# Partial-array products of a chunked scan gathered in four places a scan, and the scan's step sizes stored in another order in DRAM

## The chip, the core and the metric

The kernel runs on one core of a Trainium2 chip. The core has five engines with an instruction stream each: TensorE (PE in the profile, with its weight loads as PEld), VectorE (DVE), ScalarE (ACT), GpSimd (POOL), and SyncE (SP), whose stream issues most of the DMAs. An engine works through its stream in order; between engines, semaphores hold an instruction back until its inputs are there. PSUM, which the products are written to, is used here as eight banks of 128 x 512 float32. The metric is the device time of one execution in microseconds. The kernel before takes 1631.19 us, the median of three runs (1631.13 to 1631.39).

## What is computed

The reference is one inference step of a two-layer trunk: a Mamba-2 layer with a chunked state-space scan, and a layer of causal pooling. It takes 1024 new tokens of one prompt and 8 sequences of 8 tokens (the sample), 1088 tokens in all. The change touches the scan of the first layer and the work around it. Cut to what matters:

```python
def ssd_scan(x, dt, A, B, C, h0):          # T = 128 tokens a chunk, 8 groups of 4 heads
    acum = jnp.cumsum(dt * A, axis=2)       # cumulated step sizes within a chunk
    decay = jnp.where(mask, jnp.exp(acum[:, :, :, None] - acum[:, :, None, :]), 0.0)
    CB = jnp.einsum('bctgn,bcsgn->bctsg', C, B)
    xdt = x * dt[..., None]
    y_intra = jnp.einsum('bctsgr,bcsgrp->bctgrp', CB[..., None] * decay, xdt)
    chunk_states = jnp.einsum('bctgn,bctgr,bctgrp->bcgrpn', B, jnp.exp(acum[:, :, -1:] - acum), xdt)
    # h_c = exp(acum_end) * h_(c-1) + chunk_states_c
    y_inter = jnp.einsum('bctgn,bctgr,bcgrpn->bctgrp', C, jnp.exp(acum), h_prev)
    return y_intra + y_inter, h_final
...
mod = silu(c) @ ada_w[i] + ada_b[i]         # shift, scale, gate: the conditioning
gated = y * silu(z)                         # RMS norm over each group of 256 channels, then @ w_out
x = x + (1.0 + gate) * out
```

## The kernel before

Activations lie with channels on the 128 partitions and tokens along the free dimension. A large float32 product is done as three products of rounded parts (`mm1`, L180): high by high, high by low, low by high. 1088 tokens are cut into three pieces `CH` of 364, 364 and 360; one piece of one output tile over 8 input tiles is a *unit* of 24 products.

**The scan layer** (`ssd_layer`, L1458) runs eight scans, one for each group g of four heads. `scan_group` (L504) is a generator: each `yield` is a place where other work may be put between its steps. The other work comes from the generator `beside` (L1494): the projections of the groups in `BESIDE` (`proj_group`, L387; 12 units for one group), then the output product (`op_units`, L1523). `FILL[g]` says how many units follow each of the eleven steps of scan g. What a scan has left after eleven steps (`rest`) is drawn in the next scan, at its steps 0 and 3.

**One scan** has eight chunks of 128 tokens and a ninth, the sample's 64 tokens. They are named by what they call:

- `load_ac(c)` (L524) loads the cumulated step sizes of the group's four heads for chunk c to all 128 partitions (tile `acb`, two buffers), from the DRAM tensor `acd`. `acd` has the layout of the computation, 128 rows of 320: row 32 j + head holds chunks 2 j and 2 j + 1, so four heads of one chunk are four rows of 128 numbers with a step between them.
- `front(c)` (L534): ScalarE takes exponents from `acb`; TensorE makes C by B and three transposes into one bank `tr` (two buffers); VectorE makes the masked decay `M` and the scaled rows `xd`; ScalarE copies B's transpose (`Bt`).
- `states(c)` (L583): for a pair of chunks, two products into bank `S` (one buffer). Then twice in a row: GpSimd scales the last state (`hd`, L596) and VectorE adds the product (`h`, L597; L593 for the very first). The second state of a pair depends on the first.
- `rows(c)` (L600): the outputs of the pair into two banks `y`: products of `xd` and `M` (L609), and, where there is a state, of the state and `ea` (L613), each on half of the array's columns (128*64 in the profile), two heads side by side. VectorE adds them to the rows in place (`evac_y`, L578).
- `sample_inter` (L617): the sample's states, loaded by `load_h0`, times C on quarters of the columns (128*32; `Z`, L628, bank `S`). `back_sample` (L635): the sample's rows on 64*64 and 128*64 (L641, L644, banks `y`). `state_sample` (L656): the sample's new states on the full array (L663).
- The end: gating with z, sums of squares on quarters of the columns (`ms`, L708, bank `y`), logarithm and exponent on ScalarE, a store and a broadcast load of the factors, scaling and a store of the rows.

The step order is: `front(0)`; `front(1)`; then for each pair `states`, the next pair's first `front`, `rows`, a yield, the second `front`, a yield. The sample's Z comes with the last pair, and its rows one step later.

**The conditioning.** `ada_block` (L240) makes a block of 256 outputs: 16 instructions on quarters of the columns (L253, bank `tr`), a ScalarE copy, and after a yield a gathering product on the full array (L262). 16 of these blocks lie in the scans. `run` (L1236) plans 14 of them (`ada_plan`) to the projection units: block by block at tiles 1, 2 and 3 of each group, the first part after the second unit of the tile and the second part after the third. Two more go to the output product (`ada_late`). Their weights come through the same stream of tiles as the projection's weights, in the order of use (`items`).

**What sets the order.** The program names an order; a planner with a time model then puts each engine's instructions in the order in which their inputs are ready by that model, earlier lines of the program first. `issue_after(ins)` keeps what is traced in its block behind `ins` on that engine; `high_priority(n)` lets a block count as n places earlier; a manual dependency of class Sync makes an instruction wait for another one.

Of the kernel before, what the change touches and what calls it, by code (L numbers as in the profile page):

```python
# [50 lines left out]
FILL = (((1,) * 10 + (2,),) * 4 + ((1,) * 9 + (4, 5),) + ((3, 2, 2, 2, 2, 2, 2, 2, 2, 2, 3),) * 2 + ((2, 2, 2, 1, 1, 1, 1, 1, 2, 2, 1),))  # L51
# [46 lines left out]
class Build:  # L98
# [81 lines left out]
    def mm1(self, ps, w, k, act, ch, first, last):  # L180
        nc, (hi, lo), (ah, al), (a, n) = self.nc, w, act, ch
        nc.tensor.matmul(ps[:, :n], hi[:, k, :], ah[:, a:a + n], start=first, stop=False)  # L182
        nc.tensor.matmul(ps[:, :n], hi[:, k, :], al[:, a:a + n], start=False, stop=False)  # L183
        nc.tensor.matmul(ps[:, :n], lo[:, k, :], ah[:, a:a + n], start=False, stop=last)  # L184
# [55 lines left out]
    def ada_block(self, src):  # L240

# [56 lines left out]

    def ln_set(self, mm=None):

        ins = self.nc.scalar.preload_act_table_set("natural_log_exp_and_others")
        if mm is None:
            self.tc.keep_in_program_order(ins)
        else:
            self.tc.add_manual_dep(ins.ins, mm.ins.name, mybir.DependencyInfo(mybir.DependencyClass.Sync, mybir.DependencyReason.DATA), reason="ln_set")
# [81 lines left out]
    def proj_group(self, G):  # L387

        for ii in range(4):
# [17 lines left out]
            ada = self.ada_do(self.ada_plan[G["g"], ii]) if (G["g"], ii) in self.ada_plan else iter(())  # L407
            for c in range(3):
# [3 lines left out]
                if c:  # L412
                    next(ada, None)
# [25 lines left out]
    def dt_phase(self, ps):  # L439
# [33 lines left out]
        nc.sync.dma_start(self.acd, ac)  # L473
# [30 lines left out]
    def scan_group(self, g, T):  # L504
# [16 lines left out]
        h = [None]  # L521
        acbs = {}

        def load_ac(c):  # L524
            if c < 8:
                j, cc = c // 2, c % 2
                t = gp.tile([P, 4, 128], F32, tag="acb", bufs=2, name=self.name("acb"))
                nc.sync.dma_start(t, self.acd[32 * j + 4 * g:32 * j + 4 * g + 4, 128 * cc:128 * cc + 128].unsqueeze(0).to_broadcast([P, 4, 128]))
            else:
                t = gp.tile([P, 4, 128], F32, tag="acb", bufs=2, name=self.name("acb"))[:, :, :64]  # L530
                nc.sync.dma_start(t, self.acd[96 + 4 * g:100 + 4 * g, 256:320].unsqueeze(0).to_broadcast([P, 4, 64]))
            acbs[c] = t

        def front(c):  # L534
# [9 lines left out]
            pt = pp.tile([P, 512], F32, tag="tr", bufs=2, name=self.name("tr"))  # L544
            nc.tensor.matmul(pt[:L, 384:384 + L], B[:, tok], C[:, tok], start=True, stop=True)
            for i, t in enumerate((xs[0], xs[1], B)):
                o = pt[:, 128 * i:128 * i + 128]
                if c < 8:
                    nc.tensor.transpose(o, t[:, tok], self.ident)  # L549
                else:  # L550
                    self.dup(o, t[:, tok])
# [31 lines left out]
        def states(c, F):  # L583
# [5 lines left out]
            for i in range(2):  # L589
                cd, Si = F[i][5], S[:, 256 * i:256 * i + 256]  # L590
                hn = gp.tile([P, 4, 64], F32, tag="h", bufs=3, name=self.name("h"))
                if h[-1] is None:
                    nc.vector.tensor_copy(hn.rearrange("p r q -> p (r q)"), Si)  # L593
                else:
                    hd = gp.tile([P, 4, 64], F32, tag="hd", bufs=1, name=self.name("hd"))
                    nc.gpsimd.tensor_tensor(out=hd, in0=h[-1], in1=cd.unsqueeze(2).to_broadcast([P, 4, 64]), op=ALU.mult)  # L596
                    nc.vector.tensor_tensor(out=hn, in0=hd, in1=Si.rearrange("p (r q) -> p r q", r=4), op=ALU.add)  # L597
                h.append(hn)

        def rows(c, F):  # L600

            py = [pp.tile([P, 512], F32, tag="y", bufs=2, name=self.name("y")) for _ in range(2)]
            for i in range(2):
                tok, M, xdt, _, _, _, ct = F[i]
                hc, a = h[-3 + i], 128 * i
                for q in range(2):
                    for rr in range(2):
                        r, o = 2 * q + rr, slice(64 * rr, 64 * rr + 64)
                        nc.tensor.matmul(py[q][o, a:a + 128], xdt[:, r, :], M[:, r, :], start=True, stop=(hc is None))  # L609
                    if hc is not None:  # L610
                        for rr in range(2):
                            r, o = 2 * q + rr, slice(64 * rr, 64 * rr + 64)
                            nc.tensor.matmul(py[q][o, a:a + 128], hc[:, r, :], ct[:, r, :], start=False, stop=True)  # L613
            for q in range(2):
                evac_y(py[q], q, slice(128 * c, 128 * c + 256), 256)

        def sample_inter():  # L617

# [4 lines left out]
            nc.gpsimd.tensor_copy(mv[:, :, 1, 8:16], cv[:, :, 1, :])  # L623
            Z = pp.tile([P, 512], F32, tag="S", bufs=1, name=self.name("Z"))
# [5 lines left out]
            zsc = gp.tile([P, 4, 64], F32, tag="hd", bufs=1, name=self.name("zsc"))  # L630
# [4 lines left out]
        def back_sample(F, zsc):  # L635
            tok, M, xdt, xde, Bt, _, ea = F
            for q in range(2):
                py = pp.tile([P, 512], F32, tag="y", bufs=2, name=self.name("y"))
                for rr in range(2):
                    r, o = 2 * q + rr, slice(64 * rr, 64 * rr + 64)  # L640
                    nc.tensor.matmul(py[o, :64], xdt[:64, r, :], M[:64, r, :64], start=True, stop=False)  # L641
                for rr in range(2):
                    r, o = 2 * q + rr, slice(64 * rr, 64 * rr + 64)
                    nc.tensor.matmul(py[o, :64], zsc[:, r, :], self.kc[:, K_SEL64:K_SEL64 + 64], start=False, stop=True)  # L644
                evac_y(py, q, tok, 64)
# [28 lines left out]
        for c in range(0, 8, 2):  # L674
            states(c, F)
            if c == 6:
                load_z()
            Fn = [front(c + 2)]
            if c == 6:
                self.slots.free(B)  # L680
            rows(c, F)
            F = Fn
            if c == 6:
                zsc = sample_inter()
                self.slots.free(C)
# [6 lines left out]
        F, h = F[0], h[-1]  # L692
        nc.sync.dma_start(self.io["hpT"][g], h.rearrange("p r q -> p (r q)"))
        st = back_sample(F, zsc)
# [1112 lines left out]
```

## Time and profile before

| | |
|---|---|
| median of three runs | 1631.19 us |
| the profiled execution | 1633.98 us |
| its span, first to last instruction | 1632.2 us |
| granted TensorE clock over the span | 0.994 |
| projection and gating ahead of the scans | 0 to 354 us |
| the eight scans, with projection and output product beside them | 354 to 950 us |
| the rest | 950 to 1632 us |

How to read the profile: times are microseconds unless marked ns. L613 is line 613 of the kernel. `out<-in` names the tile that is written and those that are read, by the program's names. 128*64 is the part of the array that a product uses, rows by columns, and 128x128 the shape that it writes; a float32 product that is not split by the program shows as two instructions. Products are pipelined, so that two neighbours overlap, and the time that one takes is read from the distance of two starts. `<-` in a wait names what ended it.

### The profile page before, as it was taken

What the parts mean: (1) busy time and instruction counts of PE and PEld (TensorE: products, weight loads), DVE (VectorE), ACT (ScalarE), POOL (GpSimd) and SP (SyncE); (2) the same over time, 40 slices, a digit from 0 to 9 for tenths busy, and PEclk for the clock granted to TensorE, in tenths of its full rate; (3) what the DMA queues carried; (4) which work ended last, traced back from release to release, by engine and by line L of the source; (5) the groups of instructions that cost most, each with busy time, mean ns of one, the idle gap of its engine ahead of it and who ended that gap; (6) DMA issues with size and microseconds to landing.
All of it is one profiled execution on the core that took longest, in us unless ns stands there. A gap on an engine that the chain in (4) does not pass through costs nothing.

```text
span 1632.2 us, 30956 instructions
## 1 busy us (share of the span) xinstructions
PE 1601.1 (98%) x12061; PEld 1524.7 (93%) x12061; DVE 1290.3 (79%) x2140; ACT 816.7 (50%) x1565; POOL 495.2 (30%) x527
## 2 busy tenths in 40 slices
PE   8999999999999999999999999999999999999997
PEld 6899999998899888988998899999999999999997
DVE  6875779777788888789887867988889867577876
ACT  6653334456776767575645536632322333333364
POOL 0233556511221202121212222366667640000241
PEclk9999999999999999999999999999999999999999
DMA  9422232264555554668898533043333369565783
GB/s 346 163 98 84 93 109 71 105 203 133 183 162 167 165 186 135 217 232 299 276 332 284 201 137 111 29 142 112 102 112 99 129 213 367 166 170 173 167 164 119
DMA packets 122306, 275.60 MB, mean 169 GB/s; under 512 B 18192, under 2 KB 59312, under 8 KB 122160
## 3 DMA queue, kind: packets, MB, share of 16 engines
q1 hardware_dynamic: 118128, 260.91, 46.8%
q0 software_dynamic: 4032, 12.72, 4.5%
q8 instruction: 95, 1.56, 0.4%
q14 instruction: 51, 0.42, 0.1%
HBM read 201.12 MB, written 70.23 MB: 166 GB/s over the span
## 4 chain that ended last, share of the span: by engine, by line
PE 82%; DVE 7%; DMA 5%; issue 3%; ACT 2%; POOL 1%; SPq 0%; DVEq 0%; ACTq 0%; POOLq 0%
PE st L982 11%; PE st L980 11%; PE st L981 11%; PE mm L182 10%; PE mm L184 10%; PE mm L183 10%; DMA acb<-acd 2%; PE op L1197 2%; PE op L1198 2%; PE op L1196 2%; PE y L609 2%; PE S L588 2%; PE y L613 2%; PE am L253 1%; PE tr L549 1%
## 5 line engine op out<-in xcount | busy, mean ns | idle before, releaser
L982 PE MATMUL st<-hh,w 128*128 128x272 f32 x832 | 240.8, 289 | 2.3 <-DVE w L176 2.3
L980 PE MATMUL st<-hh,w 128*128 128x272 f32 x832 | 240.2, 289 | 0.0
L981 PE MATMUL st<-hl,w 128*128 128x272 f32 x832 | 239.7, 288 | 0.0
L982 PE MATMUL st<-t,w 128*128 128x272 f32 x624 | 179.6, 288 | 0.0
L980 PE MATMUL st<-t,w 128*128 128x272 f32 x624 | 179.6, 288 | 0.0
L981 PE MATMUL st<-t,w 128*128 128x272 f32 x624 | 179.2, 287 | 0.0
L182 PE MATMUL mm<-hh,wh 128*128 128x364 f32 (+1 forms) x528 | 178.4, 338 | 0.1
L184 PE MATMUL mm<-hh,wl 128*128 128x364 f32 (+1 forms) x528 | 174.6, 331 | 0.0
L183 PE MATMUL mm<-hl,wh 128*128 128x364 f32 (+1 forms) x528 | 173.7, 329 | 0.0
L174 ACT ACTIVATE w<-wr 128x512 fp32r<-128x512 f32 x104 | 65.6, 631 | 190.4 <-PE st L982 156.8
L982 PEld LDWEIGHTS st<-hh,w 128*128 128x128 f32 x832 | 156.4, 188 | 3.4 <-DVE w L176 3.4
L980 PEld LDWEIGHTS st<-hh,w 128*128 128x128 f32 x832 | 156.7, 188 | 0.3 <-issue 0.3
L981 PEld LDWEIGHTS st<-hl,w 128*128 128x128 f32 x832 | 156.8, 188 | 0.0
L596 POOL TENSOR_TENSOR hd<-h,cd 128x256 f32<-128x256 f32 x56 | 47.1, 842 | 353.6 <-DVE h L597 195.4
L182 PE MATMUL mm<-gh,wh 128*128 128x364 f32 (+1 forms) x384 | 130.2, 340 | 2.1 <-ACT raw L419 2.1
L1197 PE MATMUL op<-b,w 128*128 128x272 f32 x448 | 129.0, 288 | 1.3 <-DVE b L1126 1.3
L1198 PE MATMUL op<-b,w 128*128 128x272 f32 x448 | 129.0, 288 | 0.7 <-DVE w L1170 0.7
L1196 PE MATMUL op<-b,w 128*128 128x272 f32 x448 | 129.6, 289 | 0.0
L184 PE MATMUL mm<-gh,wl 128*128 128x364 f32 (+1 forms) x384 | 127.1, 331 | 0.0
L183 PE MATMUL mm<-gl,wh 128*128 128x364 f32 (+1 forms) x384 | 126.7, 330 | 0.1
L980 PEld LDWEIGHTS st<-t,w 128*128 128x128 f32 x624 | 117.7, 189 | 0.0
L982 PEld LDWEIGHTS st<-t,w 128*128 128x128 f32 x624 | 117.3, 188 | 0.0
(293 smaller groups left out, 4613.7 us busy)
## 6 DMA issues: line engine op xcount, KB each, us to landing
wr<-win SPq DMA_DIRECT2D x48, 512.0 KB, 3.7
acb<-acd SPq DMA_DIRECT2D x64, 256.0 KB, 3.9
wr<-pin SPq DMA_DIRECT2D x32, 512.0 KB, 3.6
wr<-pout SPq DMA_DIRECT2D x28, 512.0 KB, 3.9
x<-x1d SPq DMA_DIRECT2D x24, 544.0 KB, 6.3
x1d<-x SPq DMA_DIRECT2D x22, 544.0 KB, 5.4
wr<-pout POOLq DMA_DIRECT2D x20, 512.0 KB, 5.5
x<-xT SPq DMA_DIRECT2D x16, 544.0 KB, 6.0
```

Of the source, the lines that this page charges most:

```text
L174: self.nc.scalar.activation(hi, src, AF.Copy)
L182: nc.tensor.matmul(ps[:, :n], hi[:, k, :], ah[:, a:a + n], start=first, stop=False)
L183: nc.tensor.matmul(ps[:, :n], hi[:, k, :], al[:, a:a + n], start=False, stop=False)
L184: nc.tensor.matmul(ps[:, :n], lo[:, k, :], ah[:, a:a + n], start=False, stop=last)
L588: nc.tensor.matmul(S[:, 256 * i:256 * i + 256], Bt, xde.rearrange("p r q -> p (r q)"), start=True, stop=True)
L596: nc.gpsimd.tensor_tensor(out=hd, in0=h[-1], in1=cd.unsqueeze(2).to_broadcast([P, 4, 64]), op=ALU.mult)
L980: nc.tensor.matmul(ps[c][:, :QUART], hi[:, k], xh[:, t], start=(k == 0), stop=False)
L981: nc.tensor.matmul(ps[c][:, :QUART], hi[:, k], xl[:, t], start=False, stop=False)
L982: nc.tensor.matmul(ps[c][:, :QUART], lo[:, k], xh[:, t], start=False, stop=(k == 3))
L1196: nc.tensor.matmul(ps[:, :QUART], hi[:, k], xh, start=k == 0, stop=False)
L1197: nc.tensor.matmul(ps[:, :QUART], hi[:, k], xl, start=False, stop=False)
L1198: nc.tensor.matmul(ps[:, :QUART], lo[:, k], xh, start=False, stop=k == 7)
```

## The change

It has four parts.

1. *Places for the products on a part of the array.* `rows` becomes `visit`. It comes one yield after `states`, and holds, in one block with `high_priority(400)`: the row products of the pair, the first of which waits by a manual dependency for the later of the pair's two states, and behind the last of them (`issue_after`) whatever else of that kind there is. In visit 0 that is the sums of squares of the scan before (`next(rest)`), in visit 4 the sample's transposes, its C by B and Z, in visit 6 the sample's rows, and in visits 0, 2 and 6 of the first five scans a block of conditioning.
2. *What this moves.* The sample's front follows in the step of visit 4, before the last pair's states; its states are loaded at pair 2 instead of pair 4. B and C are freed there too. The sample's rows and the sums of squares go to bank `S`, the scaled Z to the tile `xl`. The second part of a conditioning block follows the next `states`. The end of a scan has two more yields, and is drawn at steps 0, 3 and 5 and in visit 0 of the next scan.
3. *The start of a scan.* From scan 1 on, the units of the first step come before the scan's first `front`, which is kept behind the last product of them, and in scans 1 to 4 the three units of the first three steps stand there together.
4. *The step sizes in DRAM.* `acd` becomes 8 chunks x 32 heads x 128, written by four DMAs, and the sample's part a tensor of its own, `acs`, written by a fifth. A load reads the four heads of a chunk as one run of 512 numbers for each partition.

```diff
-FILL = (((1,) * 10 + (2,),) * 4 + ((1,) * 9 + (4, 5),) + ((3, 2, 2, 2, 2, 2, 2, 2, 2, 2, 3),) * 2 + ((2, 2, 2, 1, 1, 1, 1, 1, 2, 2, 1),))
+FILL = ((1,) * 10 + (2,),) + (((3, 0, 0) + (1,) * 7 + (2,),) * 3 + ((3, 0, 0) + (1,) * 6 + (4, 5),) + ((3, 2, 2, 2, 2, 2, 2, 2, 2, 2, 3),) * 2 + ((2, 2, 2, 1, 1, 1, 1, 1, 2, 2, 1),))
+ADA = (0, 2, 6)
+HIGH = 400
...
+    def behind(self, ins, other):
+        self.tc.add_manual_dep(ins.ins, other.ins.name, mybir.DependencyInfo(mybir.DependencyClass.Sync, mybir.DependencyReason.DATA), reason="behind")
...
-        nc.sync.dma_start(self.acd, ac)
+        for j in range(4):
+            nc.sync.dma_start(self.acd[2 * j:2 * j + 2].rearrange("c h t -> h c t"), ac[32 * j:32 * j + 32, :256].rearrange("h (c t) -> h c t", c=2))
+        nc.sync.dma_start(self.acs, ac[96:128, 256:320])
...
-                nc.sync.dma_start(t, self.acd[32 * j + 4 * g:32 * j + 4 * g + 4, 128 * cc:128 * cc + 128].unsqueeze(0).to_broadcast([P, 4, 128]))
+                src = self.acd[c, 4 * g:4 * g + 4]
...
+            nc.sync.dma_start(t.rearrange("p r t -> p (r t)"), src.rearrange("r t -> (r t)").unsqueeze(0).to_broadcast([P, t.shape[1] * t.shape[2]]))
...
-        def rows(c, F):
+        def visit(c, F, F8=None, zsc=None):
             py = [pp.tile([P, 512], F32, tag="y", bufs=2, name=self.name("y")) for _ in range(2)]
...
+            with self.tc.high_priority(HIGH):
+                mm = None
+                for i in range(2):
...
+                            m = nc.tensor.matmul(py[q][o, a:a + 128], xdt[:, r, :], M[:, r, :], start=True, stop=(hc is None))
+                            if mm is None:
+                                mm = m
+                                self.behind(mm, hins[-1])
...
+                with self.tc.issue_after(m.ins):
+                    if c == 0:
+                        next(rest, None)
+                    if c == 4:
+                        self.pts = pp.tile([P, 512], F32, tag="tr", bufs=2, name=self.name("tr"))
+                        for i, t in enumerate((xs[0], xs[1], B)):
+                            self.dup(self.pts[:, 128 * i:128 * i + 128], t[:, NP:TOK])
+                        nc.tensor.matmul(self.pts[:64, 384:448], B[:, NP:TOK], C[:, NP:TOK], start=True, stop=True)
+                        Z = sample_products()
+                    if c == 6:
+                        _, M, xdt, _, _, _, _ = F8
+                        py8 = pp.tile([P, 512], F32, tag="S", bufs=1, name=self.name("y"))
...
+                    if (g, c) in self.ada_plan:
+                        self.ada = self.ada_do(self.ada_plan[g, c])
+                        next(self.ada)
...
         for c in range(0, 8, 2):
             states(c, F)
-            if c == 6:
+            next(self.ada, None)
+            if c < 6:
+                Fn = [front(c + 2)]
+            if c == 2:
+                load_h0()
+                sample_prep()
+            elif c == 6:
                 load_z()
...
             yield
             if c < 6:
-                F.append(front(c + 3))
+                zsc = visit(c, F)
+                Fn.append(front(c + 3))
+                F = Fn
                 if c == 4:
-                    load_h0()
+                    F8 = front(8)
+                    self.slots.free(B, C)
+            else:
+                py = visit(c, F, F8, zsc)
...
-        places = [(g, ii) for g in BESIDE for ii in (1, 2, 3) if (g, ii) != (BESIDE[-1], 3)]
+        places = [(g, c) for g in range(len(BESIDE)) for c in ADA]
...
             for i, n in enumerate(FILL[g]):
-                next(sc)
+                if i or not g:
+                    next(sc)
                 for j in range(n):
                     next(self.fill)
-                    if i in (0, 3) and j == 0:
+                    if i in (0, 3, 5) and j == 0:
                         next(rest, None)
+                if g and not i:
+                    with self.tc.issue_after(self.last_mm.ins):
+                        next(sc)
```

More of the change, by code (lines that the diff above doesn't have):

```diff
@@ L304, in ln_set @@
         else:
[L305 removed]
+            self.behind(ins, mm)
         return self.tc.issue_after(ins.ins)
@@ L633, in sample_inter, with back_sample @@
             return zsc
-        def back_sample(F, zsc):
+        def back_sample(F, py):
             tok, M, xdt, xde, Bt, _, ea = F
             for q in range(2):
[L638 to L645, printed above, removed]
+                evac_y(py[:, 64 * q:64 * q + 64], q, tok, 64)
             for i in range(2):
@@ L1479, in ssd_layer @@
         self.out_unit()
-        next(rest)
+        for _ in range(3):
+            next(rest)
         for _ in range(2):
```

95 lines of the change are left out of this document (50 added, 45 removed).

## The prediction

> **What bounds the kernel now.** I read the page first, for the engine that sets the time.
>
> ```profile
> span 1632.2 us, 30956 instructions
> PE 1601.1 (98%) x12061; PEld 1524.7 (93%) x12061; DVE 1290.3 (79%) x2140; ACT 816.7 (50%) x1565; POOL 495.2 (30%) x527
> ```
>
> TensorE is busy for 98% of the span, so time is gained only by giving TensorE less to do or less to wait for. The diff touches the eight scans, from 354 to 950 us, so next I cut that part into scans, and asked what TensorE waited for there (columns of the first view: stretch, its length, busy time and instructions of PE, PEld, DVE, ACT, POOL, clock, DMA share, GB/s).
>
> ```profile
> 435.00:510.40 75.40, 75.40 (x588) 67.78 (x586) 61.88 (x95) 51.49 (x116) 13.72 (x27) 1.00 0.51 167
> 882.00:950.00 68.00, 63.49 (x479) 57.57 (x479) 51.57 (x102) 33.52 (x79) 11.28 (x12) 0.97 0.59 204
> PE S L588 <- ACT Bt L566: 4.5, 3, 2.3
> PE mm L182 <- ACT raw L419: 2.1, 1, 2.1
> PE y L613 <- DVE h L593: 1.4, 1, 1.4
> ```
>
> The first row is scan 1, with TensorE busy all through; the second is scan 7. All its waits in the eight scans are three groups, 8.0 us: one at the first products of scan 0, one at the end of scan 4, three in scan 7. But a busy TensorE is not at its peak, so I went on to the timeline, where the distance between two starts shows what a product really takes (columns: start, duration, then the instruction; x8 is eight merged).
>
> ```profile
> 449.56 0.33 PE L184 MATMUL mm<-hh,wl 128*128 128x364 f32 x1
> ...
> 453.06 0.33 PE L184 MATMUL mm<-hh,wl 128*128 128x364 f32 x1
> ...
> 458.94 0.32 PE L183 MATMUL mm<-hl,wh 128*128 128x364 f32 x1
> 459.19 0.66 PE L613 MATMUL y<-ea,h 128*64 128x128 f32 x8
> 459.78 0.43 PE L184 MATMUL mm<-hh,wl 128*128 128x364 f32 x1
> 460.05 0.33 PE L182 MATMUL mm<-hh,wh 128*128 128x364 f32 x1
> ...
> 469.01 0.39 PE L613 MATMUL y<-ea,h 128*64 128x128 f32 x4
> 469.23 0.39 PE L609 MATMUL y<-M,xd 128*64 128x128 f32 x4
> ```
>
> From 449.56 to 453.06 lie 21 full-array products: 3.50 / 21 = 0.167 us each. In the middle of a long stretch of half-array products four of them take 469.23 - 469.01 = 0.22 us, so eight take 0.44. The eight at 459.19 stand alone in a run of full-array products, and the border shows three times: they start 0.25 after L183 instead of 0.167 (0.085 lost), take 0.59 instead of 0.44 (0.15 lost), and the first full product after them takes 0.27 instead of 0.167 (0.10 lost). **A stretch of products on a part of the array costs about 0.34 us by its two borders**, whatever is in it, and TensorE counts as busy meanwhile.
>
> **How many stretches.** Here is scan 1, which runs from one set of sums of squares (L708) to the next, by the first row of each stretch.
>
> ```profile
> 435.20 0.67 PE L708 MATMUL ms<-z,ones 128*32 128x272 f32 x8
> 444.44 0.65 PE L609 MATMUL y<-M,xd 128*64 128x128 f32 x6
> 445.65 0.87 PE L609 MATMUL y<-M,xd 128*64 128x128 f32 x10
> 446.82 0.66 PE L613 MATMUL y<-ea,h 128*64 128x128 f32 x8
> 454.72 0.44 PE L609 MATMUL y<-M,xd 128*64 128x128 f32 x4
> 459.19 0.66 PE L613 MATMUL y<-ea,h 128*64 128x128 f32 x8
> 461.14 1.07 PE L253 MATMUL am<-wr,scp 128*32 128x256 f32 x16
> 468.74 0.44 PE L609 MATMUL y<-M,xd 128*64 128x128 f32 x4
> 479.36 1.07 PE L253 MATMUL am<-wr,scp 128*32 128x256 f32 x16
> 481.42 0.27 PE L545 MATMUL tr<-xbc,xbc 128*64 128x64 f32 x1
> 489.55 0.33 PE L641 MATMUL y<-M,xd 64*64 64x64 f32 x4
> 499.71 1.07 PE L253 MATMUL am<-wr,scp 128*32 128x256 f32 x16
> ```
>
> That is 12. Counted the same way along the timeline, scan 0 has 11, scans 1 to 3 have 12 each, scan 4 has 11, scan 5 has 11 (its first pair alone is in four), scans 6 and 7 have 6 each, and the squares of the last scan stand alone: 11 + 36 + 11 + 11 + 12 + 1 = 82, from the first row here to the last.
>
> ```profile
> 366.65 0.66 PE L609 MATMUL y<-M,xd 128*64 128x128 f32 x8
> ...
> 942.07 0.67 PE L708 MATMUL ms<-z,ones 128*32 128x272 f32 x8
> ```
>
> **The change part by part.**
>
> *Gathering.* After it, each scan has four visits, 32 in all. The squares go into the next scan's first visit, the conditioning products (L253) into visits 0, 2 and 6 of scans 0 to 4 (15 blocks, 14 before), the sample's transposes and Z into visit 4, the sample's products (L641, L644) into visit 6. Outside stay the squares of scan 7 and one late conditioning block: 34 stretches. No product is added or dropped. Removed: 82 - 34 = 48 borders, 48 x 0.34 = **-16.3 us**.
>
> *Changes of shape inside a visit.* A visit that goes from halves (128*64) to quarters (128*32) pays there. Before, this already happens once a scan, between the row products and Z:
>
> ```profile
> 483.45 0.48 PE L609 MATMUL y<-M,xd 128*64 128x128 f32 x4
> 483.67 0.48 PE L613 MATMUL y<-ea,h 128*64 128x128 f32 x4
> 484.08 1.07 PE L628 MATMUL Z<-h,ctm 128*32 128x256 f32 x16
> 485.08 0.43 PE L182 MATMUL mm<-hh,wh 128*128 128x360 f32 x1
> ```
>
> Four halves take 0.22 (483.45 to 483.67), the last four 0.41; part of the 0.19 is the tail that any stretch pays at its end, and I take 0.13 as the price of the change. New ones: three in each of scans 0 to 4 (squares and conditioning have the same shape), one in each of scans 5 to 7: 18 x 0.13 = **+2.3 us**. The sample's products are now entered from halves instead of from the full array; at 0.05 each, between nothing and the price of a change, 8 x 0.05 = **+0.4 us**. Bounds for both: 0 and 18 x 0.19 + 8 x 0.13 = 4.5.
>
> [...]
>
> *Waiting for the last state.* The first product of a visit waits for the later of the pair's two states (`behind`), and all the rest of the visit, and every full product issued after it, queues behind it on TensorE. Before, only L613 waited, and for the earlier state. The states of the pair at 453 us come at
>
> ```profile
> 458.36 0.41 DVE L597 TENSOR_TENSOR h<-hd,S 128x256 f32<-128x256 f32 x1
> 461.18 0.41 DVE L597 TENSOR_TENSOR h<-hd,S 128x256 f32<-128x256 f32 x1
> ```
>
> so the row products of that pair move from 454.72 to after 461.6. What covers this is the projection beside the scan, 4.0 us a unit (24 x 0.167), which the planner places ahead because it is ready; the visit's priority only brings it forward once its inputs are planned to be there. From 420 to 700 us the waits of TensorE have no row at all, with L613 placed in the middle of a unit (459.19) as soon as its state was done, so the planner's times hold against VectorE's. The evictions (L580) come later by the same 7 us; states do not read them, so the next pair doesn't wait. I take **0**, with bounds 0 and one POOL and one DVE step a visit (below).
>
> *Scan starts.* Scans 1 to 7 now have their fill of the first three steps first and then two fronts, the states and a third front. Units are the same in number: 12 in scans 1 to 3, 18 in scan 4. The front's loads and ScalarE work can run under those units (12 us). I take 0; without that cover a scan would stand for one landing, 3.9 us.
>
> *PSUM and slots.* The squares, the sample's rows and Z share the one bank "S" with the states; the next states come two units, 8 us, later, and between them lies one evicting step of ScalarE or VectorE. The load of the sample's states moves two steps ahead on SP's queue, past two loads of step sizes; if a slot is late, these and ScalarE queue behind it. Cover: each of those loads is issued a chunk ahead. 0; without it one landing, 3.9 us, once.
>
> *Step sizes in DRAM.* The store is five issues in place of one, in the front, before the scans begin: 0. Each load reads 2 KB in one run a partition instead of four of 512 B.
>
> ```profile
> acb<-acd SPq DMA_DIRECT2D x64, 256.0 KB, 3.9
> hpT<-h SPq DMA_DIRECT2D x8, 128.0 KB, 3.0
> ACT cd L574 <- DMA acb<-acd: 9.6, 3, 4.9
> ```
>
> A landing takes 3.9 us; a transfer of half the bytes in runs of 1 KB takes 3.0, so I expect 3.0 to 3.9. This pays only in scan 7, where ScalarE waits for these loads (last row, 846 to 950 us) and TensorE then for ScalarE, three times: 0 to 3 x 0.9 = 2.7 us less. I take the middle, **-1.3 us**. [...]
>
> **Sum.** -16.3 + 2.3 + 0.4 - 1.3 = -14.9 us. The profiled execution took 1633.98 us (1632.2 of it span), so 1619; the median of the runs is 2.8 below it, so **1616 us**.
>
> **The rivals.** *Visits that are a little late.* The borders (12 x 0.34 = 4.1 us in scan 1) have so far given VectorE time to get a state done; with fewer of them this slack shrinks. At 0.25 us a visit, 32 x 0.25 = 8: 1624. For it: VectorE is busy 61.9 of 75.4 us in order; against it: the empty list of waits.
>
> *Slower: every visit waits for the second state.* Place: the new wait of a visit's first product. Price: if TensorE reaches it when the first state is done, it stands for the second's GpSimd and VectorE steps, 0.61 (POOL row below) + 0.41 = 1.0 us, 32 x 1.0 = 32: 1616 + 32 = 1648. It decides above 14.9 / 32 = 0.47 us a visit. For it: the two states above are 2.8 us apart. Against: TensorE has other ready work, and the wait is planned.
>
> ```profile
> 458.85 0.61 POOL L596 TENSOR_TENSOR hd<-h,cd 128x256 f32<-128x256 f32 x1 [8.97 <-DVE h L597]
> ```
>
> *Not gathered.* The planner still puts full products between the parts of a visit, since conditioning waits for its weights and row products for their own inputs. With two of three removed borders back, -16.3 becomes -5.4 and the sum -4; with all back, 1631. Against it: every extra is tied behind the visit's last row product. I put 1629.
>
> *The old waits go too.* If the 4.5 in scan 7 disappear, and with them its slow clock (0.97 of 68 us, 2 us), and the waits of 2.1 and 1.4: 10.0 instead of 1.3, so 1607. Against it: they come from loads and an eviction that the change hardly touches.
>
> **How the numbers follow.** Forecast 0.60; a little late 0.20; slower 0.08; not gathered 0.06; old waits gone 0.06. The range goes from 1608 to 1628: it takes in the forecast with its bounds (-16.3 + 4.5 = -11.8 at one end, -16.3 - 2.7 = -19 at the other, so 1612 to 1619), the late visits up to 0.4 us each, and most of the last case. A change under 0.2%, 3.3 us, can't be told from none. Faster: 0.60 + 0.20 + 0.06 and a third of "not gathered", 0.88; within: 0.04; slower: 0.08.
>
> **What would show it.** In the profile after: about 34 stretches, scans 1 to 3 shorter by 8 x 0.34 - 3 x 0.13 = 2.3 us each, 73.1 instead of 75.4, with TensorE still busy throughout and no row for waits of L609 on L597 or L593; the same spacing of 0.22 for four halves; loads of step sizes landing in under 3.9. A row "L609 waits for h" of over 8 us would show the late visits, of over 15 the slower case. Wrong would be the forecast if scans 1 to 3 stayed at 75 us with no wait shown: then the borders are not what costs.

## The result

The changed kernel takes 1645.88 us, the median of four runs (1644.65 to 1652.7), beside 1631.29 us before (1631.13 to 1633.79): a ratio of 1.0094 with a 95% interval from 1.0065 to 1.0124. Forecast were 1616 us. The ratios below leave out three executions that were far slower than the others of their kernel: one of `e3` (1692.9 us), one of `e10` (5458.9 us) and one of the kernel before (2208.6 us). The profiled execution took 1652.7 us, slower than the median; a reading of where its extra 7 us lie follows below. First its page, the span and the busy times:

```profile
span 1650.9 us, 30957 instructions
PE 1601.8 (97%) x12061; PEld 1532.4 (93%) x12061; DVE 1297.2 (79%) x2140; ACT 812.4 (49%) x1564; POOL 505.3 (31%) x527
```

TensorE has as many products as before (12061) and is as long busy (1601.1 us before), in a longer span (1632.2 us before): it waits. The waits of TensorE in the scans after the change (total, times, longest):

```profile
PE y L622 <- DVE h L605: 14.8, 16, 2.2
PE S L596 <- ACT Bt L574: 6.9, 5, 2.1
PE mm L184 <- DVE gs L812: 1.4, 1, 1.4
PE S L701 <- ACT xs L698: 1.0, 1, 1.0
PE S L596 <- DVE zsc L676: 0.5, 1, 0.5
PE mm L184 <- ACT raw L423: 0.3, 1, 0.3
```

That is 24.9 us instead of 8.0, and the first row is new: L622 is the first product of a visit (L609 before), L605 the later state (L597 before). Scans 1 to 3, from one set of sums of squares to the next, in the same view as before:

```profile
460.80:541.90 81.10, 78.83 (x590) 71.28 (x586) 63.35 (x95) 50.83 (x118) 18.39 (x27) 0.94 0.47 156
541.90:618.90 77.00, 74.54 (x590) 67.75 (x586) 62.93 (x95) 50.49 (x118) 18.57 (x27) 1.00 0.51 165
618.90:697.00 78.10, 75.83 (x590) 69.23 (x586) 63.02 (x95) 50.75 (x118) 18.39 (x27) 0.98 0.49 162
```

Each of them was 75.4 and was to become 73.1. Counted along the timeline as before, there are 34 stretches of products on a part of the array, exactly as forecast. So the gathering was done, and it did not pay.

**Where the wait comes from.** The longest waits stand at the last visit of a scan. This is scan 1 after, TensorE, with the wait in brackets:

```profile
494.33 0.44 PE L622 MATMUL y<-M,xd 128*64 128x128 f32 x4 [1.95 <-DVE h L605]
...
495.25 0.39 PE L622 MATMUL y<-M,xd 128*64 128x128 f32 x4
495.47 0.47 PE L629 MATMUL y<-ea,h 128*64 128x128 f32 x4
495.72 0.65 PE L622 MATMUL y<-M,xd 128*64 128x128 f32 x4
496.15 0.65 PE L629 MATMUL y<-ea,h 128*64 128x128 f32 x4
```

VectorE in the same microseconds, in its order:

```profile
487.16 0.68 DVE L570 TENSOR_TENSOR xd<-tr,tkx 128x512 f32<-128x512 f32 x1
487.76 1.62 DVE L568 TENSOR_TENSOR M<-M,cb 128x512 f32<-128x512 f32 x1
489.31 2.43 DVE L583 TENSOR_TENSOR ea<-xbc,ea 128x512 f32<-128x512 f32 x1
...
492.72 0.40 DVE L605 TENSOR_TENSOR h<-hd,S 128x256 f32<-128x256 f32 x1
...
493.85 0.42 DVE L605 TENSOR_TENSOR h<-hd,S 128x256 f32<-128x256 f32 x1 [0.53 <-POOL hd L604]
```

And GpSimd:

```profile
486.89 4.29 POOL L685 TENSOR_TENSOR h<-h,ea 128x1024 f32<-128x1024 f32 x2
493.20 0.61 POOL L604 TENSOR_TENSOR hd<-h,cd 128x256 f32<-128x256 f32 x1 [2.02 <-DVE h L605]
```

The two operations `M` and `ea` take 0.69 us each where nothing lies beside them (rows of `e3` below), and here 1.62 and 2.43. They lie beside the two scalings of the sample's states on GpSimd (L685, 486.89 to 491.18), and the last pair's states, which follow in VectorE's order, come 2.7 us late. `xd`, which reads one input from PSUM, took its usual 0.68 beside the same work (0.67 to 0.69 in all 72). Each of the two slow ones ends shortly after a scaling: the scalings take 1.94 and 2.39 us, and `M` ends at 489.38, 0.55 us after the first, and `ea` at 491.74, 0.56 us after the second. What holds the two back until then is not shown by a row.

Before, the same scaling started when the last states were done (481.60 and 482.75 in the rows of VectorE). GpSimd and VectorE of the kernel before:

```profile
485.29 4.52 POOL L647 TENSOR_TENSOR h<-h,ea 128x1024 f32<-128x1024 f32 x2 [0.26 <-issue]
```

```profile
481.60 0.42 DVE L597 TENSOR_TENSOR h<-hd,S 128x256 f32<-128x256 f32 x1 [0.70 <-PE S L588]
482.75 0.42 DVE L597 TENSOR_TENSOR h<-hd,S 128x256 f32<-128x256 f32 x1 [0.73 <-POOL hd L596]
...
486.03 1.98 DVE L575 TENSOR_TENSOR ea<-xbc,ea 128x512 f32<-128x512 f32 x1
```

An `ea` beside it took 1.98 us there too, and ended 0.54 us after the first scaling (2.18 us, to 487.47), but nothing of the running pair came after it. The change traces the sample's front in the step of visit 4, so its `ea`, which the scaling needs, is ready before the last pair's states instead of behind them.

**The clock.** In the visit above, four products follow each other at 0.22 us (495.25 to 495.47) and then at 0.43 (495.72 to 496.15). A window of the kernel after from the wait on shows a granted clock of 0.58:

```profile
494.30:506.50 12.20, 12.17 (x87) 10.10 (x88) 7.82 (x13) 5.93 (x15) 1.36 (x4) 0.58 0.60 188
```

About 10 us at half clock followed this wait (12.20 x 0.42 / 0.5), and shorter pieces followed those of scans 3 and 4 (a clock of 0.98 over scan 3, and of 0.83 from 730 to 740 us). The wait alone does not bring it: the one of 1.97 us in scan 2 of this execution was followed by full clock (1.00 over the scan), and so were the three of 1.95 and 1.96 us in scans 1 to 3 of `e2` (below; 0.995 over its span). In the other three runs the mean clock is 0.991 to 0.994 instead of 0.988, and they are 6 to 8 us faster: the time of the profiled execution above the median goes with these pieces.

### The profile page after: what moved, and what is told of

The parts are those of the page before. It is cut to its first block, busy times and chain, and to the rows that moved or that the text cites. A ratio compares the mean times of both kernels' runs of the same rounds, so it can differ in the third digit from the quotient of the medians.

```text
span 1650.9 us, 30957 instructions
## 1 busy us (share of the span) xinstructions
PE 1601.8 (97%) x12061; PEld 1532.4 (93%) x12061; DVE 1297.2 (79%) x2140; ACT 812.4 (49%) x1564; POOL 505.3 (31%) x527
## 4 chain that ended last, share of the span: by engine, by line
PE 74%; DVE 11%; DMA 5%; issue 5%; ACT 3%; POOL 1%; SPq 0%; DVEq 0%; ACTq 0%; POOLq 0%
PE st L1027 11%; PE st L1025 11%; PE st L1026 11%; PE mm L185 8%; PE mm L184 8%; PE mm L186 8%; PE op L1242 2%; PE op L1243 2%; PE op L1241 2%; PE y L622 1%; DMA gr<-gyd 1%; DMA wr<-win 1%; PE am L256 1%; DVE M L568 1%; PE y L629 1%
## 5 line engine op out<-in xcount | busy, mean ns | idle before, releaser
L185 PE MATMUL mm<-hl,wh 128*128 128x364 f32 (+1 forms) x528 | 177.8, 337 | 0.0
L184 PE MATMUL mm<-hh,wh 128*128 128x364 f32 (+1 forms) x528 | 177.3, 336 | 0.0
L604 POOL TENSOR_TENSOR hd<-h,cd 128x256 f32<-128x256 f32 x56 | 52.1, 930 | 280.8 <-DVE h L605 139.9
L184 PE MATMUL mm<-gh,wh 128*128 128x364 f32 (+1 forms) x384 | 129.2, 338 | 1.7 <-DVE gs L812 1.4
```

## The experiments

Ratios are to the kernel before, run in turn on the same chip, with 95% intervals.

**The layout alone, and all but the layout.** `e1_layout_only` puts the new stores, loads and DRAM tensors of the step sizes into the kernel before. `e2_old_layout` puts the old ones into the kernel after, the same lines the other way round.

```diff
# e1, in the kernel before
-        nc.sync.dma_start(self.acd, ac)
+        for j in range(4):
+            nc.sync.dma_start(self.acd[2 * j:2 * j + 2].rearrange("c h t -> h c t"), ...)
+        nc.sync.dma_start(self.acs, ac[96:128, 256:320])
```

> The kernel before with only the new order of the step sizes in DRAM (store and loads). Collision theory (GpSimd's scaling of the sample's states, planned ahead of the last pair's states, slows VectorE beside it and holds visit 6 up by 2 us a scan) and wait theory (any visit pays for waiting for the later state): the layout is not the cause, so within 3 us of before, 1628 to 1634. Layout theory (loads of step sizes land in 4.6 us instead of 3.9 and make the fronts late): slower by 5 us or more, landing over 4.3.

> The changed kernel with the old order of the step sizes in DRAM. Collision and wait theory: within 4 us of the changed kernel, 1642 to 1650, visit 6 still waiting about 2 us in scans 0 to 4. Layout theory: 1640 or less.

Measured: 1.0000 [0.9989, 1.0011] and 1.0081 [1.0062, 1.0100]. The layout costs or brings nothing beyond the 1.8 us of its interval. On the page of the kernel after, the median load (`acb<-acd`) lands in 4.6 us, where it took 3.9 before: the landing became longer, not shorter. In the old program the new layout lands in 4.1 (`e1`), and in the new program the old layout lands in 4.7 (`e2`). So the rest of the change moved it, not the length of the runs; that it is the place of the loads in time is not shown.

**The scaling of the sample's states kept behind the last pair's states.**

```diff
# e3, in the kernel after: hds collects the instructions of L604
-            for i in range(2):
-                nc.gpsimd.tensor_tensor(out=h0[i], in0=h0[i], ...)
+            with self.tc.issue_after(hds[-1].ins):
+                for i in range(2):
+                    nc.gpsimd.tensor_tensor(out=h0[i], in0=h0[i], ...)
```

> The changed kernel with GpSimd's two scalings of the sample's states kept behind the last pair's second scaling on GpSimd's queue. Collision theory: the waits of visit 6 in scans 0 to 6 (12.4 us in the profile) go, and the half clock behind them, so 1633 or less, down to 1626. Wait theory: the list of waits of L622 for the states stays at over 12 us and the time over 1642.

Measured: 1.0028 [1.0010, 1.0045], so about 11 us of the 15 are gone with one line on GpSimd's order (the median, 1634.61, is 1.6 above what the collision theory allowed). VectorE of `e3` at the same place in scan 1:

```profile
484.62 0.69 DVE L568 TENSOR_TENSOR M<-M,cb 128x512 f32<-128x512 f32 x1
485.21 0.69 DVE L583 TENSOR_TENSOR ea<-xbc,ea 128x512 f32<-128x512 f32 x1
```

TensorE's waits for the later state fall from 14.8 to 4.0:

```profile
PE y L622 <- DVE h L605: 4.0, 11, 0.8
```

The collision is shown as the cause of most of the loss. It is moved rather than gone: the scalings now lie beside a rounding of weights (`wl`, L142, at 490.33), which takes 2.59 us in place of 1.22, and no wait of TensorE on it is shown. But with the states clear of it the kernel is still not faster than before, and scans 1 to 3 are where they were, with full clock:

```profile
457.70:532.90 75.20, 74.63 (x590) 67.89 (x586) 61.48 (x95) 50.61 (x118) 17.86 (x27) 1.00 0.49 169
532.90:608.60 75.70, 74.67 (x590) 67.83 (x586) 61.76 (x95) 50.37 (x118) 18.06 (x27) 1.00 0.51 168
608.60:683.80 75.20, 74.56 (x590) 67.88 (x586) 61.62 (x95) 50.59 (x118) 17.86 (x27) 1.00 0.50 168
```

So 226.1 us for the three instead of 226.2 with 24 stretches fewer, and 1.7 us of waits in them. That is close to what the prediction named as the sign that borders are not what costs, scans 1 to 3 at 75 us with no wait shown. The gain of the gathering itself is missing, and the other runs ask for it.

**No wait for the later state.**

```diff
# e4, in the kernel after
-                                self.behind(mm, hins[-1])
+                                pass
```

> The changed kernel without the manual wait for the later state, so that a product waits for its own inputs alone. Wait theory: the 14.8 us of waits go and the gathering stays worth 14, 1622 or less. Collision theory: the products of the second chunk still need the first state of the pair, which is late by the same collision, so only one step of GpSimd and VectorE (1.1 us) is saved in each of seven scans, about 1638, with some visits split.

Measured: 1.0213 [1.0196, 1.0231], 20.1 us of waits, 109 stretches. The time, 1665.52 us, is far above what either theory allowed. Without the wait the planner takes the visits apart; the wait is what keeps them whole, and it costs less than it saves.

**The wait for the earlier state.** `e5_first_state` is `e3` and `e7_first_only` the kernel after, each with this edit:

```diff
-                                self.behind(mm, hins[-1])
+                                self.behind(mm, hins[-2])
```

> The kernel with the late scaling (e3) where a visit waits for the earlier of the pair's two states, which is the only new state that its products read. Theory that the added wait is one step of GpSimd and VectorE too long: the 4.0 us of waits of L622 for the states fall under 1.5 and visits stay whole (34 to 40 stretches), 1631 or less. Rival, that the gathering needs the later state: visits split again, over 45 stretches, 1636 or more.

> The changed kernel, scaling not moved, where a visit waits for the earlier state. Collision theory: VectorE reaches the earlier state 1.1 us sooner than the later one, so the 2.0 us waits of visit 6 in scans 1 to 4 fall to 0.9 and the time to 1637 to 1641. Theory that the choice of state is the whole cause: 1633 or less.

Measured: 1.0019 [1.0003, 1.0034] and 1.0091 [1.0062, 1.0120]. With the collision still there nothing is won: the wait for the state shrinks to 2.0 us and `S <- Bt` grows to 14.8. With the states clear of the collision (`e5`) their row is down to 1.0, and a new one stands there:

```profile
PE y L645 <- DVE h L605: 4.1, 1, 4.1
```

The sample's rows (L645) share bank `S` with the states and wait until the later state has been read from it.

**The old fill.** `e6_old_fill` is `e3`, and `e8_first_old_fill` is `e5`, with the old `FILL` and the old order of step and units.

```diff
-FILL = ((1,) * 10 + (2,),) + (((3, 0, 0) + (1,) * 7 + (2,),) * 3 + ...
+FILL = (((1,) * 10 + (2,),) * 4 + ((1,) * 9 + (4, 5),) + ...
```

> The kernel with the late scaling (e3) with the old distribution of units (one a step in scans 1 to 4, the first front ahead of the units). Theory that the front-loaded units cost: the waits for ScalarE's copies (8.0 us: S for Bt and for xs) fall to 5 and the time to 1631 or less. Rival, that they are what keeps the fronts' loads hidden: 1637 or more, with new waits at the scans' starts.

> Late scaling, wait for the earlier state, old distribution of units. If each of the three is a part of the cost by itself, this is the fastest, 1628 or less; if the front-loaded units hide loads, it is slower than the run with the first two alone by 3 us or more.

Measured: 1.0080 [1.0059, 1.0101] and 1.0088 [1.0067, 1.0110]. The first is 8.5 us above `e3`, and its visits wait 10.1 us for the later state instead of 4.0: the three units ahead of a scan are cover that the visits need. The second shows that waiting for the earlier state doesn't replace this cover; at 1643.93 us it also refutes that each of the three edits gains by itself (1628 or less).

**The two leftovers of `e3`: a bank, and products standing alone.** `e9_first_other_bank` is `e5` with the sample's rows in a bank of the transposes. `e10_gather_at_states` is `e3` with the second part of a conditioning block (L265, four products of nine columns) directly behind the states. `e11_both` has both.

```diff
# e9
-                        py8 = pp.tile([P, 512], F32, tag="S", bufs=1, name=self.name("y"))
+                        py8 = pp.tile([P, 512], F32, tag="tr", bufs=2, name=self.name("y"))
# e10, in states(); the call behind states() is dropped
+            with self.tc.high_priority(HIGH), self.tc.issue_after(sm.ins):
+                next(self.ada, None)
```

> The version with the late scaling and the wait for the earlier state took 1.0019 of before and left one new wait of 4.1 us in scan 5, where the sample's rows (L645) waited for the bank that the later state had still to read. Here they get a bank of the transposes instead; the products are the same. If what is left above before is waits, this one goes: 1629 to 1630 with before at 1631 (ratio 0.999), and the row 'L645 waits for h' is gone. If what is left is products standing alone among others, the 4.1 go to another wait or come off alone and the ratio stays at 1.001 to 1.003; scans 1 to 3 stay at 74.5 to 75.2 us in either case.

> The version with the late scaling (1.0028 of before), and the conditioning's small products of nine columns (L265) issued directly behind the pair's states (L596), ahead of the transposes, instead of alone among projection products; eight or nine of some ten blocks move. Theory 'products alone': each that stood alone cost some 0.2 to 0.35 us more, so 2 to 3 us come off, 1631.5 to 1632.5 with before at 1631 (ratio 1.0005 to 1.001), and scans 1 to 3 become 0.3 to 0.7 us shorter each than 75.1, 75.7, 75.2. Theory 'only waits': the place does not matter, 1634 to 1635, ratio 1.0025 to 1.003.

> Both together on the late scaling: the earlier state is waited for, the sample's rows have a bank of the transposes, the small conditioning products stand with the states. If both costs are real and add, 1626 to 1628 with before at 1631, ratio 0.997 to 0.9985, below before; if only waits count, as the version with the other bank alone (0.999); if neither, 1.002. My forecast of the whole change stood at 0.991 and is out of reach in each case.

Measured: 1.0004 [0.9991, 1.0017], 1.0053 [1.0033, 1.0074] and 1.0009 [0.9996, 1.0021]. The 4.1 us row is gone in `e9`, which is as fast as before. In `e11` the scans 1 to 3 become shorter, as the theory of products standing alone has it:

```profile
456.40:530.40 74.00, 73.83 (x590) 67.90 (x586) 60.44 (x95) 51.08 (x118) 14.12 (x27) 1.00 0.52 171
530.40:605.20 74.80, 73.97 (x590) 67.92 (x586) 60.17 (x95) 51.15 (x118) 14.29 (x28) 1.00 0.54 170
605.20:679.30 74.10, 73.93 (x590) 67.95 (x586) 60.26 (x95) 50.68 (x118) 14.76 (x28) 1.00 0.52 170
```

That is 222.9 instead of 226.2, and 2.3 less than the 225.2 of `e9`, in which the nine-column products stand alone. But the row `S <- Bt` is 9.6 us (4.9 in `e9`), of which 7.1 lie in scans 6 and 7 (2.6), so the last scans give it back, and 1.0009 is far from the 0.997 to 0.9985 of costs that add. `e10` is against its expectation: its profiled execution, the fastest of its runs, took 1630.5, near the expected 1631.5, and the others 1633 to 1643; and scans 1 to 3 of that execution take 226.1 us, no less than in `e3`, with 2.5 us of waits in place of 1.7. So the gain from moving the nine-column products is seen in `e11` alone. No version beats the kernel before.

**What an interruption costs.** The kernel before, with one extra product that nobody reads, at 57 places in the middle of the 24 projection products of a chunk: on the whole array (`e12_extra_full`) and on half of it (`e13_extra_half`).

```diff
-                self.mm3(ps, w, self.hn, CH[c])
+                for k, act in enumerate(self.hn):
+                    self.mm1(ps, w, k, act, CH[c], k == 0, k == 7)
+                    if k == 3:
+                        nc = self.nc
+                        nc.tensor.matmul(ps[:, 400:409], self.ident, self.kc[:, K_SEL9:K_SEL9 + 9], start=False, stop=False)
# e13: ps[:64, 400:409] and self.ident[:, :64]
```

> The kernel before, with one extra product on the whole array (128x9, nobody reads it) put between the twelfth and the thirteenth of the 24 projection products of 57 chunks in the scans. It measures what an interruption of the projection costs without any change to a part of the array. Theory 'every interruption costs' (the 0.1 us at the return is paid after any other product, whatever its shape): 0.25 to 0.35 us each by the lone blocks of nine columns (four take 0.36, the first projection product after them 0.08 more), 57 x 0.3 = 17 us, ratio 1.009 to 1.012. Theory of the prediction (only a stretch on a part of the array has a border): no more than its own 0.03 to 0.1 us, 2 to 6 us, ratio 1.001 to 1.004.

> The same with the extra product on half of the array (128*64, nine columns). Both theories put a border here: by the prediction's 0.34 us and its own 0.03, 57 x 0.37 = 21 us, ratio 1.013. What tells them apart is the difference to the extra product on the whole array: 57 x 0.09 = 5 us if only the late start in front of a part of the array is special to it, 15 us or more if the border is a matter of the array's shape alone.

Measured: 1643.40 and 1652.86 us beside 1632.87, ratios 1.0075 [1.0050, 1.0100] and 1.0126 [1.0100, 1.0152]: 10.5 / 57 = **0.185 us for an interruption on the whole array, 20.0 / 57 = 0.35 on half of it**. By the intervals of the ratios it is 0.14 to 0.29 and 0.29 to 0.44. Both expectations were missed: `e12` lies between its two ranges, nearer to that of 'every interruption costs', and the difference of 9.5 us lies between 5 and 15. The 0.03 us that both expectations take for the product itself was the author's estimate and is shown by no run. The timeline of `e12`:

```profile
402.98 0.33 PE L184 MATMUL mm<-hh,wl 128*128 128x364 f32 x1
403.14 0.28 PE L414 MATMUL mm<-kc 128*128 128x9 f32 x2
403.28 0.41 PE L182 MATMUL mm<-hh,wh 128*128 128x364 f32 x1
403.53 0.33 PE L183 MATMUL mm<-hl,wh 128*128 128x364 f32 x1
```

and of `e13`:

```profile
404.98 0.33 PE L184 MATMUL mm<-hh,wl 128*128 128x364 f32 x1
405.24 0.28 PE L414 MATMUL mm<-kc 128*64 128x9 f32 x2
405.45 0.43 PE L182 MATMUL mm<-hh,wh 128*128 128x364 f32 x1
405.72 0.33 PE L183 MATMUL mm<-hl,wh 128*128 128x364 f32 x1
```

From L184 to L183 lie 0.55 and 0.74 us, where two projection products alone take 0.33. The 0.22 and 0.41 us more are above the prices from the times. TensorE's waits in the scans, 4.7 and 5.5 us in these profiles and 8.0 before, are lower by about as much as 57 such differences. The late return (403.28 to 403.53, 405.45 to 405.72: 0.25 and 0.27 instead of 0.167) is the same in both; what only the half array has is the late start (404.98 to 405.24) and 0.07 us more for the product itself. The weight loads of `e13` show the late start as a load that starts 0.25 us after the product before it, which began at 404.98:

```profile
404.82 0.19 PEld L184 LDWEIGHTS mm<-hh,wl 128*128 128x128 f32 x1
405.23 0.19 PEld L414 LDWEIGHTS mm<-kc 128*64 128x64 f32 x2 [0.23 <-issue]
```

while in `e12` it starts with it, at 402.98:

```profile
402.82 0.19 PEld L184 LDWEIGHTS mm<-hh,wl 128*128 128x128 f32 x1
402.98 0.35 PEld L414 LDWEIGHTS mm<-kc 128*128 128x128 f32 x2
```

**The account.** An *interruption* is a place in the scans where something else stands between two products of the projection or the output product, counted along the timeline. With 0.17 us for a stretch on a part of the array (0.35 - 0.185), 0.19 for an interruption, the prediction's 2.7 us for the shapes inside visits, and the waits of each profile (8.0 before), the differences to before come out as follows. The sums of e4 and e10 lie clearly outside the measured intervals, and that of e6 just outside.

| | stretches | interruptions | waits, us | worked out, us | measured, us (ratio x 1631) |
|---|---|---|---|---|---|
| before | 82 | 120 | 8.0 | | |
| after | 34 | 133 | 24.9 | -8.2 + 2.5 + 2.7 + 16.9 = +13.9 | +15.3 [10.6, 20.2] |
| e3 | 34 | 132 | 14.9 | -8.2 + 2.3 + 2.7 + 6.9 = +3.7 | +4.6 [1.6, 7.3] |
| e4 | 109 | 167 | 20.1 | 4.6 + 8.9 + 2.7 + 12.1 = +28.3 | +34.7 [32.0, 37.7] |
| e6 | 34 | 127 | 21.7 | -8.2 + 1.3 + 2.7 + 13.7 = +9.5 | +13.0 [9.6, 16.5] |
| e9 | 38 | 129 | 10.1 | -7.5 + 1.7 + 2.7 + 2.1 = -1.0 | +0.7 [-1.5, 2.8] |
| e10 | 34 | 124 | 13.6 | -8.2 + 0.8 + 2.7 + 5.6 = +0.9 | +8.6 [5.4, 12.1] |
| e11 | 34 | 118 | 16.6 | -8.2 - 0.4 + 2.7 + 8.6 = +2.7 | +1.5 [-0.7, 3.4] |

Worked out in the same way, `e2`, `e5`, `e7` and `e8` come to +11.9, +1.8, +11.3 and +12.8 us, beside +13.2, +3.1, +14.8 and +14.4 measured, all within their intervals.

Two things limit the account. The waits are those of one execution each (`e1`, as fast as before, has 5.7 us in place of 8.0). And not every interruption costs 0.19 us. The sample's new states, products of 128x512 on the whole array (L702 in `e3`), start on time, and the projection behind them keeps its 0.17:

```profile
501.22 0.33 PE L186 MATMUL mm<-hh,wl 128*128 128x364 f32 x1
501.39 0.39 PE L702 MATMUL S<-xs,Bt 128*128 128x512 f32 x1
...
501.85 0.33 PE L184 MATMUL mm<-hh,wh 128*128 128x364 f32 x1
502.02 0.33 PE L185 MATMUL mm<-hl,wh 128*128 128x364 f32 x1
```

Counted along the timeline, 9 of the 120 interruptions before and 21 of the 133 after are of these products alone. If they are free, 111 and 112 are left that cost, the 2.5 us in the row of the kernel after shrink to 0.2 and its sum to +11.6; e3 comes to +1.6, and e9, at -2.9, falls out of its interval. So the account holds to some 5 us, not finer, and leaves e4 and e10 open.

## Why the prediction was wrong

**Waiting for the last state: 0 forecast, 14.8 us measured.** This is the larger miss. The step followed the pair's own chain, and named the projection as its cover. It did not follow the sample's front, which the diff moves in front of the last pair's states, to the two GpSimd operations that become ready with it. They come before the states and slow two VectorE operations on the way to them by 2.7 us. `e3` shows it: 11 us. Per visit it is 14.8 / 32 = 0.46, at the 0.47 from which the slower rival was to decide; that rival had the place, but not the mechanism, and 16 waits are shown, not 32. The announced sign, a row over 8 for late visits and over 15 for the slower case, puts the 14.8 with the late visits, just short of the slower case. That the slower rival's 1648 lies near the measured 1645.88 is luck: it had 32 us of waits on top of the full border gain.

**Borders: -16.3 forecast, about -8.2, and at most 2.5 of it given back.** The failed sentence is "a stretch of products on a part of the array costs about 0.34 us by its two borders, whatever is in it". The price is right for what it was measured on, a stretch alone among projection products (0.35 in `e13`). But about 0.185 of it is paid for a short product on the whole array too (`e12`), and the rows show the late return also behind transposes, though not behind the sample's states. Most of the 82 stretches stood next to other products: of the 120 interruptions before, 22 hold products on a part of the array alone, 50 hold such products beside others, and 48 hold others alone. After the change it is 22, 12 and 99. So where the gathering took the partial products away, the interruption by the others mostly stayed: the change has 133 for 120. A row of the kernel before could have said so: a transpose group on the whole array, with the same late return (441.89 to 442.14 is 0.25).

```profile
441.54 0.60 PE L549 MATMUL tr<-kc,xbc 128*128 128x128 f32 x4
441.89 0.41 PE L184 MATMUL mm<-hh,wl 128*128 128x360 f32 x1
442.14 0.33 PE L182 MATMUL mm<-hh,wh 128*128 128x360 f32 x1
```

In scans 1 to 3, by start distances, the time inside the stretches fell from 42.7 us to 40.3 in `e3`, as forecast (24 x 0.15 - 9 x 0.13 = 2.4); the time outside them was to fall by 24 x (0.085 + 0.10) = 4.4 and rose by 2.2, of which 1.7 are waits.

**Shapes inside a visit: +2.7, held.** The 2.4 just named contain them, and rows of `e3` show one change by itself: from the last four halves of a visit to the first quarters lie 0.31 us, where four halves take 0.22, so it costs 0.09.

```profile
466.34 0.39 PE L629 MATMUL y<-ea,h 128*64 128x128 f32 x4
466.65 1.07 PE L256 MATMUL am<-wr,scp 128*32 128x256 f32 x16
```

The prediction took 0.13 for such a change, between bounds of 0 and 0.19.

**The step sizes: -1.3 forecast, 0 measured, give or take 1.8** (`e1`). The interval does not exclude the forecast, but its step fails: the landing got no shorter (4.1 in `e1` and 4.6 in the change, for 3.9). The 3.0 us from which the lower bound was taken belong to `hpT<-h`, a store to DRAM and not a load. Scan 7's waits `S <- Bt` did shrink, from 4.5 us to 2.7 in `e1` and to 2.9 in the change, but with the old layout in the new program (`e2`) they are 2.9 as well.

**Scan starts: 0 forecast.** As a whole this can't be read off, but the front-loaded units are worth 8.5 us to the new order (`e6` against `e3`); their cover was rightly named, and not priced. **PSUM: 0 forecast, 0.5 measured** (`S <- zsc`); the shared bank cost 4.1 us only once the wait was for the earlier state (`e5`).

**The other rivals.** "Not gathered" is refuted by the 34 stretches. "The old waits go" is refuted: of the 4.5 us in scan 7, 2.9 are still there, and with new ones in scans 0 and 6 the row is 6.9. "A little late" had the sign of its cause right, but its price was added to a border gain that was not there.

## What to carry to other kernels

Before a border is priced by its shape, an interruption of the same place by a short product of the same shape as its surroundings should be priced too, and what counts is how many interruptions the long run keeps. A step that is moved earlier takes all its followers with it: ask of each, on every engine, what it now runs beside and ahead of. Where a new wait makes an engine's order stiff, what a helper engine loses can turn into a stall (here 2.7 us of VectorE in front of the last visit of scan 1, and 1.95 us of TensorE at it).

## What the runs showed of the hardware

GpSimd and VectorE were not independent: beside two 128x1024 operations of GpSimd (1.94 and 2.39 us), 128x512 operations of VectorE with both inputs in SBUF took 1.62 and 2.43 us instead of the 0.69 of `e3`, and one with an input in PSUM took its usual 0.68. A stall of TensorE of 1.95 us was followed by about 10 us at half clock in one execution (0.58 over 12.2 us), and stalls of the same length by full clock in that execution (1.00 over scan 2) and in another (`e2`, 0.995 over the span). A single product of nine columns between large ones costs 0.185 us on the whole array (0.14 to 0.29) and 0.35 on half of it (0.29 to 0.44), though in the trace of `e12` the projection's next product starts 0.14 us after it. Products of 128x512 on the whole array, in the same place, show no such loss: in `e3` one starts 0.17 us after the projection's product before it, and the projection behind it keeps its 0.17.
